# Moving the last store's completion wait to the semaphore clear, and issuing the bulk store one reduction earlier, in a row-sum kernel

## The chip, the cores and the metric

The kernel runs on one core of one Trainium2 chip. The metric is the device time of one execution in microseconds (us). Timed runs of two kernels are taken in turn on the same chip.

A timed run is about 1.8 us longer than the span that the trace shows for it. Differences inside the span carry over; the absolute numbers don't.

The views of the profile name the engines PE (TensorE), DVE (VectorE), ACT (ScalarE), POOL (GpSimd) and SP (SyncE); a q behind the name, as in SPq, means that engine's instruction queue, and L148 is line 148 of that kernel's file. A *semaphore* is a counter that some instructions change and others wait for. A transfer has *landed* when the last of the 16 additions to its semaphore is on record (for the last store of the kernel before they run from 159.983 to 160.151 us). A *barrier* is a point that every engine must reach before any of them goes on. A *drain* is a DRAIN instruction of the trace; here it matters only as an instruction that a wait can stand on. The *span* runs from the start of the first instruction in the trace to the end of the last.

## The reference

```python
batch, seq, dim = 32, 512, 1024
def reference(x):                       # x: (32, 512, 1024) float32
    return np.sum(x, axis=-1).astype(np.float32)
```

67.1 MB are read once, and 64 KB of sums are written.

## The kernel before

The 16,384 rows are cut into eight groups. In each, a partition holds 16 whole rows, so a full load is 8 MB. All loads are issued by SyncE, in order, into three buffers. VectorE reduces the groups; from the seventh group on, ScalarE takes some of the rows. The last group is loaded in shrinking pieces (8 rows, 5 rows, 2 rows, and one row in two parts) so that little work is left when the last bytes land. Results leave by two stores: the *group store* (seven groups, 896 pieces of 64 bytes, issued by ScalarE) and the *last store* (the eighth group, 128 pieces of 64 bytes, issued by SyncE).

```python
def rows(t, a, n, j, n_act, pairs=False):
    nv = n - n_act
    block = t[:, a * dim : (a + n) * dim].rearrange("p (n d) -> p n d", d=dim)
    load = nc.sync.dma_start(out=block, in_=rows_from(j, n))
    ...                                  # nv rows to VectorE, n_act rows to ScalarE
    return load
# ... groups 0 to 6 ...
rows(t, 0, 8, j, 4)
rows(t, 8, 5, j + 8, 2, pairs=True)
rows(t, 13, 2, j + 13, 1, pairs=True)    # the "two-row load"
# ...
nc.vector.memset(whole[:, width + 1 :], 0.0)
nc.sync.dma_start(out=part, in_=rows_from(j, 1)[:, 0, :c])
nc.sync.dma_start(out=whole[:, 1 : width + 1], in_=rows_from(j, 1)[:, 0, c:])
hold(store(nc.scalar, 0, last), sums_of[-1], "its packets come behind those of the loads")
halves(whole[:, :1], part)
halves(sums[:, j : j + 1], whole)
store(nc.sync, last, last + 1)
```

`hold(a, b)` makes `a` wait for `b`. So the group store waits for VectorE's sum of the two-row load.

The framework adds a closing block behind this. In the kernel before, cut to what matters:

```
SyncE    waits for every load, both stores and all engines' counts; the last
         of these waits (the last store) stands on a drain
all      first barrier: each engine's drain adds 1; GpSimd gathers 4, then releases 4
GpSimd   drain
GpSimd   clear of the semaphores
GpSimd   drain
all      second barrier, the same way
```

A second hook of the kernel, `order_waits`, only orders the waits of one instruction. It sorts the last store's wait to the front of the drain's list; in the trace that wait then stands on the drain itself (160.167 us), and the other waits on instructions ahead of it.

## Time and profile before

| | before |
|---|---|
| median of the first three runs | 162.2 us (161.96 to 162.31) |
| span of the trace | 160.9 us |
| loads, share of the chain that ended last | 73% |
| VectorE's long reductions, share of the same chain | 24% |
| last load landed to last store issued | 0.48 us |
| last store issued to landed | 1.42 us |
| last store landed to the clear | 0.365 us |
| last store landed to the end of the span | 0.75 us |

The page of the kernel before gives the span, then the chain of waits by engine and line, then groups of instructions: busy us, mean ns of one, idle time before them and what ended it.

```profile
span 160.9 us, 126 instructions
...
DMA t<-in_x_dram 73%; DVE sums L98 24%; SPq L137 1%; SPq L178 0%; DVE t L112 0%; DVEq L209 0%
...
L98 DVE TENSOR_REDUCE sums<-t 128x16 f32<-128x16384 f32 (+3 forms) x9 | 116.6, 12953 | 36.2 <-DMA t<-in_x_dram 36.2
```

The packets of SyncE's DMA queue, nearly all of them loads, take up 97.6% of the 16 DMA engines' time, so the kernel is paced by its loads; by this chain, what can still gain are the loads themselves or what comes after them.

The timeline of the kernel before shows the end (start us, duration us, engine, line, operation). Shown are VectorE's sum of the two-row load's last row, the group store on ScalarE's queue, VectorE's very last sum, and the last store on SyncE's queue.

```profile
156.96 0.69 DVE L112 CUSTOM_DVE_ANT_0 t<-t 128x512 f32<-128x512 f32 x1 [0.58 <-DMA t<-in_x_dram]
...
157.69 0.41 ACTq L148 DMA_DIRECT2D out_dram<-sums  x1
...
158.30 0.40 DVE L112 CUSTOM_DVE_ANT_0 t<-t 128x233 f32<-128x233 f32 x1
158.62 0.08 DVE L112 DVE_READ_ACCUMULATOR2_ANT sums<- 128x1 f32 x1
158.74 0.35 SPq L148 DMA_DIRECT2D out_dram<-sums  x1
```

The group store is released 0.73 us after VectorE starts on the two-row load's last sum. After the last store's issue no engine computes, yet the span goes on to 160.9: that is the store's flight and the closing block.

SyncE's waits of the kernel before (waiter, what it waited for: total us, times, longest us) say what it does there.

```profile
SPq L209 <- DMA out_dram<-sums: 0.8, 2, 0.5
SPq L209 <- PEq L209: 0.6, 2, 0.4
```

It waits for both stores ("2"), and only then enters the barriers (the second line; the view puts those waits down to TensorE's queue, but in the raw records they end behind GpSimd's release, in the first barrier at 160.378 us, 0.042 us after the release started). The views leave out the semaphore instructions of the closing block; their times below come from the raw event records of the same trace.

### The profile page before, as it was taken

Reading aid. Unit: us, or ns where it says so; the run is one execution under the profiler, and the core shown is the slowest. Engines: PE = TensorE matmul, PEld = TensorE weight load, DVE = VectorE, ACT = ScalarE, POOL = GpSimd, SP = SyncE. Lnnn points to the kernel's source line nnn. Section 1 sums busy time; section 2 is a strip of 40 time slices with the busy share of each in tenths; the row PEclk is TensorE's granted clock in tenths of the full one; section 3 lists DMA queues with packets and bytes.
Section 4 is the critical chain, followed back from the end, with each engine's and each line's share of the span. In section 5 each row is a group of like instructions: output and inputs, shape, how many; then the busy total and the mean of one; then the engine's idle time right before and its main releaser. Section 6 shows DMA issues by size and latency. Waiting matters only on the chain.

```text
span 160.9 us, 126 instructions
## 1 busy us (share of the span) xinstructions
DVE 120.1 (75%) x22; ACT 17.3 (11%) x31; POOL 0.2 (0%) x4
## 2 busy tenths in 40 slices
DVE  0280069950799958999499994999949999597943
ACT  3000000000000000000000000000000000596952
POOL 0000000000000000000000000000000000000000
DMA  7999996996996969969969969969969969999993
GB/s 265 452 477 501 391 521 261 521 521 261 521 521 261 521 261 521 521 261 521 521 261 521 521 261 521 521 261 521 521 261 521 521 261 521 391 391 424 407 406 82
DMA packets 2929, 67.18 MB, mean 418 GB/s; under 512 B 1265, under 2 KB 1393, under 8 KB 1521
## 3 DMA queue, kind: packets, MB, share of 16 engines
q1 hardware_dynamic: 2016, 67.12, 97.6%
q10 hardware_dynamic: 912, 0.06, 0.4%
q14 instruction: 1, 0.00, 0.0%
HBM read 67.11 MB, written 0.07 MB: 417 GB/s over the span
## 4 chain that ended last, share of the span: by engine, by line
DMA 73%; DVE 24%; SPq 1%; issue 0%; DVEq 0%
DMA t<-in_x_dram 73%; DVE sums L98 24%; SPq L137 1%; SPq L178 0%; DVE t L112 0%; DVEq L209 0%
## 5 line engine op out<-in xcount | busy, mean ns | idle before, releaser
L98 DVE TENSOR_REDUCE sums<-t 128x16 f32<-128x16384 f32 (+3 forms) x9 | 116.6, 12953 | 36.2 <-DMA t<-in_x_dram 36.2
L125 ACT ACTIVATE unread<-t 128x1024 f32<-128x1024 f32 x15 | 15.2, 1013 | 140.0 <-DMA t<-in_x_dram 140.0
L112 DVE CUSTOM_DVE_ANT_0 t<-t 128x512 f32<-128x512 f32 (+2 forms) x6 | 3.5, 601 | 2.4 <-DMA t<-in_x_dram 2.3
L125 ACT ACTIVATION_READ_ACCUMULATOR unread<-t 128x1 f32 x15 | 2.8, 188 | 0.0
L125 ACT ACT_TABLE_LOAD x1 | 1.3, 1283 | 0.8 <-PEq L198 0.8
L112 DVE DVE_READ_ACCUMULATOR2_ANT sums<- 128x1 f32 x5 | 0.4, 82 | 0.0
L198 POOL MEMSET const-bfloat16-1.0<- 128x1 bf16 x1 | 0.1, 102 | 0.0
L198 POOL MEMSET const-uint8-127<- 128x1 uint8 x1 | 0.1, 101 | 0.0
L198 POOL MEMSET const-float32-0.0<- 128x1 f32 x1 | 0.1, 99 | 0.2 <-issue 0.2
L198 POOL MEMSET const-float32-1.0<- 128x1 f32 x1 | 0.1, 98 | 0.0
L112 DVE DVE_READ_ACCUMULATOR2_ANT t<- 128x1 f32 x1 | 0.1, 82 | 0.0
L176 DVE MEMSET t<- 128x1 f32 x1 | 0.1, 59 | 0.0
## 6 DMA issues: line engine op xcount, KB each, us to landing
t<-in_x_dram SPq DMA_DIRECT2D x1, 6144.0 KB, 20.8
t<-in_x_dram SPq DMA_DIRECT2D x1, 4096.0 KB, 31.1
t<-in_x_dram SPq DMA_DIRECT2D x1, 2560.0 KB, 36.9
t<-in_x_dram SPq DMA_DIRECT2D x1, 2048.0 KB, 7.1
t<-in_x_dram SPq DMA_DIRECT2D x1, 1024.0 KB, 38.9
t<-in_x_dram SPq DMA_DIRECT2D x1, 280.0 KB, 39.2
t<-in_x_dram SPq DMA_DIRECT2D x1, 232.0 KB, 39.3
t<-in_x_dram SPq DMA_DIRECT2D x6, 41.2
```

The costliest lines, as they stand in the source:

```text
L98: return nc.vector.tensor_reduce(out=dst, in_=src, axis=mybir.AxisListType.X, op=mybir.AluOpType.add)
L112: return nc.vector.tensor_tensor_reduce(out=src[:, :n], in0=src[:, :n], in1=src[:, n:], scale=1.0, scalar=0.0, op0=mybir.AluOpType.add, op ...
L125: nc.scalar.activation(out=unread[:, :n], in_=src, func=mybir.ActivationFunctionType.Copy, accum_out=dst,)
L137: load = nc.sync.dma_start(out=block, in_=rows_from(j, n))
L176: nc.vector.memset(whole[:, width + 1 :], 0.0)
L198: nc = _bacc.Bacc("TRN2", target_bir_lowering=False, num_devices=1)
```

## The change

The intent is to let the first closing barrier run while the last store is still in flight. SyncE no longer waits for that store; GpSimd does, on the drain that already stands between the first barrier and the clear. The clear is kept behind the landing, because it also acts on the semaphore that the store increments (in the trace before, that semaphore changes at 160.566 us, 0.05 us after the clear starts). That a clear ahead of the landing would do harm is reasoning. The group store's hold moves from VectorE's sum to the two-row load itself, so that SyncE, which still waits for the group store ahead of the barrier, is early enough.

```diff
 def order_waits(nc):
...
-            elif isinstance(inst, mybir.InstDrain) and inst.engine == SP:
-                insts[k] = with_first(inst, stored)
...
+def wait_for_the_store_at_the_clear(nc):
+    ...                       # take `wait` (the last store) off SyncE's drain
+    insts[at] = copy.replace(
+        insts[at], sync_info=mybir.SyncInfo(on_wait=rest, on_update=info.on_update)
+    )
+    pool = [k for k, i in enumerate(insts) if i.engine == mybir.EngineType.Pool]
+    clear = next(k for k in pool if isinstance(insts[k], mybir.InstISA))
+    drain = pool[pool.index(clear) - 1]
+    ...                       # checks that this drain waits for nothing yet
+    insts[drain] = copy.replace(
+        insts[drain], sync_info=mybir.SyncInfo(on_wait=[wait], on_update=[])
+    )
...
-        rows(t, 13, 2, j + 13, 1, pairs=True)
+        two = rows(t, 13, 2, j + 13, 1, pairs=True)
...
-        hold(store(nc.scalar, 0, last), sums_of[-1], "its packets come behind those of the loads")
+        hold(store(nc.scalar, 0, last), two, "its packets come behind those of the loads")
```

The source adds no instruction to any engine.

More of the change, by code (lines that the diff above doesn't have):

```diff
@@ L42, in order_waits @@
     SP = mybir.EngineType.SP
-    stored = None
     for block in nc.main_func.blocks:
@@ L52, in order_waits @@
                 insts[k] = with_first(inst, "DVE")
-                stored = inst.sync_info.on_update[0].ant_name
-            elif isinstance(inst, mybir.InstDrain) and inst.engine == SP:
-                insts[k] = with_first(inst, stored)
         block.instructions = insts
+def wait_for_the_store_at_the_clear(nc):
+    end = nc.main_func.blocks[-1]
+    insts = list(end.instructions)
+    stored = [
+        i.sync_info.on_update[0].ant_name
+        for b in nc.main_func.blocks
+        for i in b.instructions
+        if isinstance(i, mybir.InstDMACopy) and i.engine == mybir.EngineType.SP
+    ][-1]
+    at = next(
+        k
+        for k, i in enumerate(insts)
+        if isinstance(i, mybir.InstDrain) and i.engine == mybir.EngineType.SP
+    )
+    info = insts[at].sync_info
+    (wait,) = [w for w in info.on_wait if w.ant_name == stored]
+    rest = [w for w in info.on_wait if w.ant_name != stored]
+    insts[at] = copy.replace(
[4 more added lines that the diff above has]
+    drain = pool[pool.index(clear) - 1]
+    assert isinstance(insts[drain], mybir.InstDrain)
+    info = insts[drain].sync_info
+    assert info is None or not (info.on_wait or info.on_update)
+    insts[drain] = copy.replace(
+        insts[drain], sync_info=mybir.SyncInfo(on_wait=[wait], on_update=[])
+    )
+    end.instructions = insts
 @with_exitstack
@@ L68 @@
     nc.at_finalize(order_waits)
+    nc.at_finalize(wait_for_the_store_at_the_clear)
     fp32 = mybir.dt.float32
```

## The prediction

> **What bounds the kernel now.** The chain of waits gives 73% of the 160.9 us span to the loads of x and 24% to VectorE's long reductions, which free the buffers of later loads. The change touches neither; it acts on the last 4 us only. There the raw events of the trace read: two-row load landed 156.93; last load landed 158.26; last two-piece sum on VectorE done 158.72; last store (SyncE) issued 158.74, its 128 packets 159.57 to 159.78, landed 160.15. Group store (ScalarE): issued 157.69, released by VectorE's sum at 157.67; its 896 packets 158.64 to 159.38, landed 159.80. After the last landing comes a serial tail: SyncE's drain wakes 160.17, second drain 160.23, GpSimd gathers 160.26, releases 160.34, drains 160.42, clears the semaphores 160.52, and a second barrier ends at 160.9.
>
> **What the change does.**
> 1. SyncE no longer waits for the last store, so the first closing barrier runs while that store is in flight; GpSimd's existing drain in front of the clear takes the wait. From landing to clear it was 160.516 - 160.151 = 0.365 us. What remains is the wake (0.016 us, as SyncE's drain shows) and drain to clear (160.516 - 160.417 = 0.099 us): 0.115 us. Gain 0.25 us, all on the critical path. The second barrier is paced by GpSimd before and after (the other engines' drains end at 160.55, GpSimd's gather starts 160.72), so the shift passes through whole. No instruction is added to any engine.
> 2. SyncE's wait for the group store remains, ahead of the barrier. At the old landing (159.80) SyncE would reach its barrier at about 160.0 and GpSimd its drain at about 160.19, 0.02 to 0.04 us late: the early group store covers that. In the built program the dependency on the two-row load vanishes, since ScalarE's preceding activation already waits for it; the issue follows at about 156.98, 0.71 us earlier. With the same 0.95 us from issue to first packet its packets run 157.94 to 158.66, landing near 159.1. SyncE then passes everything by about 159.45 and GpSimd stands at its wait from about 159.7, some 0.45 us ahead of the landing.
>
> **The cost to fear.** The early packets could run into the last loads: their last data packet ends at 157.81, only 0.13 us before the first expected store packet. [...] I expect none or a few hundredths. The last store's own packets meet no group packets before or after, so its 1.41 us from issue to landing should stand.
>
> **Predicted time.** 162.2 - 0.25 = 161.95 us. The three runs of before spread over 0.35 us, as much as the gain, so the 8-in-10 range is 161.6 to 162.3. Faster by over 2%: 0.005; within 2%: 0.99; slower: 0.005.
>
> **What would show each step.** Timeline of the tail: group store issued at about 157.0; SyncE's drains before 159.6; GpSimd's first gather before 159.7; its drain 0.02 us after the last landing; the clear 0.1 to 0.13 us after that landing instead of 0.37. The last load's landing should stay 1.3 us behind the two-row load's, the last store's issue to landing 1.4 us.
>
> **What would make it wrong.** [...] a drain of GpSimd that wakes more slowly from a DMA's semaphore than SyncE's; a second barrier not paced by GpSimd; or run-to-run drift of the loads, which moves more than the tail.

Two passages are cut from this text: a mechanism by which early store packets would delay the last load, with an upper bound for it, and the same mechanism in the list of what would make it wrong. No run of this case shows that mechanism. No term of the sum was in them: the forecast is 162.2 - 0.25 = 161.95 us, with nothing added for a collision. "None or a few hundredths" is what the author expected of that delay.

## The result

| | before | after |
|---|---|---|
| median of 6 runs | 162.12 us (161.94 to 162.47) | 161.91 us (161.72 to 162.35) |
| ratio | 1 | 0.9988 (95% interval 0.9971 to 1.0005) |

A ratio is the mean time of one kernel's runs over that of the other's of the same rounds, so it is not quite the ratio of the medians quoted beside it. The medians came out 0.21 us apart. These twelve runs alone do not prove a gain: the interval includes 1.

The same page lines for the changed kernel (all line numbers have moved by the inserted code, L98 to L130 and so on):

```profile
span 160.2 us, 125 instructions
...
DMA t<-in_x_dram 73%; DVE sums L130 24%; SPq L169 1%; SPq L210 0%; DVE t L144 0%; DVEq L241 0%
...
L130 DVE TENSOR_REDUCE sums<-t 128x16 f32<-128x16384 f32 (+3 forms) x9 | 116.6, 12953 | 35.5 <-DMA t<-in_x_dram 35.5
```

The span is 0.65 us shorter, more than was predicted, and a reader should not book all of it: the long reductions are just as busy (116.6 us) but waited 0.7 us less for loads, which the change does not touch. (0.3 us of that comes back in front of the sums of the last small pieces, whose waits grew from 2.3 to 2.6 us, so the loads as a whole were about 0.4 us faster.) The traced execution of the kernel before was also a slow one of its kind: it took 162.69 us, more than any of its six timed runs.

The timeline of the changed kernel:

```profile
156.56 0.69 DVE L144 CUSTOM_DVE_ANT_0 t<-t 128x512 f32<-128x512 f32 x1 [0.58 <-DMA t<-in_x_dram]
156.62 0.41 ACTq L180 DMA_DIRECT2D out_dram<-sums  x1
...
157.88 0.40 DVE L144 CUSTOM_DVE_ANT_0 t<-t 128x233 f32<-128x233 f32 x1
158.21 0.08 DVE L144 DVE_READ_ACCUMULATOR2_ANT sums<- 128x1 f32 x1
158.32 0.35 SPq L180 DMA_DIRECT2D out_dram<-sums  x1
```

The group store now leaves 0.06 us after the two-row load's sum has started (0.73 us before). The last stretch, from VectorE's last half to the last store, is 0.44 us in both.

SyncE's waits of the changed kernel in the closing block:

```profile
SPq L241 <- PEq L241: 1.1, 2, 0.9
```

The line that waited for `out_dram` is gone. SyncE now waits longer inside the barriers (0.6 to 1.1 us): it is there early.

The raw event records of the two traces, in us from the start of each span:

| event | before | after |
|---|---|---|
| five-row load landed | 154.42 | 154.02 |
| two-row load landed | 156.93 | 156.54 |
| last load landed | 158.26 | 157.84 |
| group store: issued, packets, landed | 157.69, 158.64 to 159.38, 159.80 | 156.62, 157.54 to 158.28, 158.72 |
| last store: issued, packets, landed | 158.74, 159.57 to 159.78, 160.151 | 158.32, 159.16 to 159.37, 159.744 |
| SyncE's drain of the first barrier | 160.23 | 159.04 |
| GpSimd gathers, releases | 160.26, 160.34 | 159.07, 159.15 |
| GpSimd's drain in front of the clear starts | 160.417 | 159.768 |
| the clear starts | 160.516 | 159.867 |
| end of the span | 160.899 | 160.250 |

Of the last store's 1.42 us in the kernel before, 0.84 us pass from the start of the issue to the first packet (0.49 us from its end), 0.21 us are packets, and 0.37 us pass from the last packet to the landing.

Four terms add up to the 0.65 us. The last load landed 0.417 us earlier; the way from there to the last store's issue took 0.002 us more; the store's flight took 0.008 us more; landing to end fell from 0.748 to 0.506 us, by 0.242 us. The first term is not the change's: 0.40 of the 0.417 us was already there when the five-row load landed, before either edit acts. Over the thirteen traces the last load lands anywhere from 157.42 to 158.26 us.

### The profile page after: what moved, and what is told of

The parts are those of the page before. It is cut to its first block, busy times and chain, and to the rows that moved or that the text cites. A ratio compares the mean times of both kernels' runs of the same rounds, so it can differ in the third digit from the quotient of the medians.

```text
span 160.2 us, 125 instructions
## 1 busy us (share of the span) xinstructions
DVE 120.1 (75%) x22; ACT 17.3 (11%) x31; POOL 0.2 (0%) x4
## 4 chain that ended last, share of the span: by engine, by line
DMA 73%; DVE 25%; SPq 1%; issue 0%; DVEq 0%
DMA t<-in_x_dram 73%; DVE sums L130 24%; SPq L169 1%; SPq L210 0%; DVE t L144 0%; DVEq L241 0%
## 5 line engine op out<-in xcount | busy, mean ns | idle before, releaser
L130 DVE TENSOR_REDUCE sums<-t 128x16 f32<-128x16384 f32 (+3 forms) x9 | 116.6, 12953 | 35.5 <-DMA t<-in_x_dram 35.5
```

Of the source, the lines that this page charges most:

```text
L130: return nc.vector.tensor_reduce(out=dst, in_=src, axis=mybir.AxisListType.X, op=mybir.AluOpType.add)
```

## The experiments

Two measures carry the verdicts: the *tail*, from the last landing of a store to the clear and to the end of the span, and the ratio to the kernel before. All kernels gave the correct result. Each kernel was timed six times, three of them (the group store late, among the last loads, and earlier still) four times. The kernel before ran 11 times on each of three chips, beside the kernels of that chip.

### The kernel before against itself

No edit.

> The kernel before against itself, on one chip with the three runs that follow. Every theory expects a ratio of 1.000; how far it is off, and how wide its interval is, says what a difference of 0.15% in the others is worth. In its trace the last landing comes 0.365 us before the clear, as in the first profile, while the landing of the last load may move by 0.4 us, as it did between the two profiles, if that is drift.

Measured: 162.31 us against 162.03 us, ratio 1.001 (0.999 to 1.003). Landing to clear 0.366 us, landing to end 0.749 us. The last load landed at 157.91 us, 0.34 us earlier than in the first trace of the very same kernel. So the loads drift by nearly as much as the unexplained part of the spans, and a single ratio from some six runs is good to about 0.2% either way. The tail repeats to 0.001 us.

### The change again, twice

No edit.

> The change again, in more rounds. My theory (the gain is the barrier taken out from behind the last landing): landing to clear 0.12 us against 0.365 us, 0.24 us off the time, a ratio of 0.9985. Rival (the 0.2 us between the medians is drift of the loads, which landed 0.4 us earlier in the second profile): a ratio of 1.000.

> The change a third time, beside the next run on one chip. Landing to clear 0.12 us, landing to end 0.51 us in its trace; ratio to the kernel before 0.9985 by the tail alone, with an interval of some 0.15% to either side.

Measured: ratios 0.9991 (0.9972 to 1.0009) and 0.9977 (0.9961 to 0.9994). In both traces landing to clear is 0.123 us and landing to end 0.506 us. With 0.9988 of the first comparison, the three ratios have a mean of 0.9985, which is 0.24 us of 162.2. Two of the three intervals include 1; taken together as independent, they give an estimate of about 0.9975 to 0.9995 for the mean. The rival, drift alone, does not explain the tail, and it would put all three ratios below 1 only one time in eight.

### The wait at the clear alone

```diff
-        hold(store(nc.scalar, 0, last), two, ...)
+        hold(store(nc.scalar, 0, last), sums_of[-1], ...)
```

> The wait at the clear alone; the group store stays behind VectorE's sum. My theory: group store lands 0.35 us before the last store, SyncE then needs 0.19 us to its barrier and GpSimd 0.19 us more to its drain, which is 0.03 us after the last landing: landing to clear 0.15 us, 0.21 us off the time, ratio 0.9987. Rival (the early group store is what gains): landing to clear as before, ratio 1.000.

Measured: landing to clear 0.161 us, landing to end 0.544 us, ratio 0.9993 (0.9971 to 1.0016), too wide to decide. The tail decides: this half of the change gives 0.205 of the 0.243 us. SyncE's waits of this kernel show what still holds it:

```profile
SPq L241 <- DMA out_dram<-sums: 0.6, 1, 0.6
```

One wait is left, for the group store, which landed at 159.07, 0.35 us before the last store (159.42). From there GpSimd's drain started at 159.479, 0.062 us after the last landing instead of 0.024 us in the change.

### The early group store alone

The kernel before, with its hold moved to `two`.

> The early group store alone; SyncE's drain waits for the last store as before. My theory: nothing is gained, landing to clear 0.365 us, issue of the last store to its landing 1.41 us, ratio 1.000. Rival (the early group store clears the way of the last store): issue to landing under 1.3 us and a ratio of 0.9985 or so.

Measured: landing to clear 0.366 us, landing to end 0.749 us, last store 1.414 us from issue to landing, ratio 1.0001 (0.9984 to 1.0018). SyncE's waits of this kernel:

```profile
SPq L209 <- DMA out_dram<-sums: 0.7, 1, 0.7
```

Again one wait, but this time for the last store. The early store by itself buys nothing. Together with the moved wait it is worth 0.544 - 0.506 = 0.038 us.

### The group store held until VectorE's last sum

```diff
-        hold(store(nc.scalar, 0, last), two, ...)
         halves(whole[:, :1], part)
-        halves(sums[:, j : j + 1], whole)
+        total = halves(sums[:, j : j + 1], whole)
+        hold(store(nc.scalar, 0, last), total, ...)
```

> The wait at the clear as in the change, but the group store held until VectorE's last sum, so issued beside the last store. My theory: the group store is still waited for ahead of the first closing barrier, so it now lands last, about 2.1 us after its issue, and the whole barrier comes behind it: landing of the group store to clear 0.45 to 0.5 us, 0.9 to 1.1 us slower than the change, ratio to the kernel before 1.004 to 1.006. Rival (with the wait at the clear the group store's time no longer matters): ratio 0.9985.

Measured: 162.98 us, ratio 1.005 (1.0033 to 1.0066). SyncE's waits of this kernel:

```profile
SPq L241 <- DMA out_dram<-sums: 1.7, 1, 1.7
```

Both stores were issued at 157.91; the last store landed at 159.38, the group store at 160.07. The whole first barrier came behind the group store: 0.509 us from its landing to the clear, 0.892 us to the end. So the wait that the change left on SyncE still counts: the tail got shorter where the group store landed 1.02 us (the change) or 0.35 us (the run with the wait alone) ahead of the last one, and longer here, where it landed 0.69 us behind it. The 0.509 us was 0.01 us over what was expected.

### The group store among the last loads

```diff
-        rows(t, 8, 5, j + 8, 2, pairs=True)
+        five = rows(t, 8, 5, j + 8, 2, pairs=True)
+        hold(store(nc.scalar, 0, last), five, ...)
...
-        hold(store(nc.scalar, 0, last), two, ...)
```

> The change with the group store issued about 1.1 us earlier still, on ScalarE ahead of the two-row load's activation. My theory: its 56 packets of 10 ns on each DMA engine now run among the last loads' packets, and the last load lands 0.3 to 0.9 us later against the five-row load's landing (3.9 us before), of which 0.55 us is the packets' own time: ratio 1.001 to 1.004. Rival (small packets slip in between for nothing, so the order never mattered): the last load's landing stays within 0.1 us and the ratio is that of the change, 0.9985.

Measured: 162.15 us, ratio 1.0003 (0.9983 to 1.0024). The timings from the five-row load's landing say more: the last load's data packets end 3.42 us later, inside the 3.32 to 3.43 us of the kernels with the store behind the loads, but it *lands* 3.956 us later, against 3.804 to 3.835 us there. Sorted in order of time, its 16 completion packets (of 4 bytes) took 0.61 us from packet to landing on average, against 0.44 to 0.50 us there. So there is a cost, of 0.12 to 0.15 us, and it is smaller than the 0.3 us or more that I expected. The rival (under 0.1 us) misses too, by little.

Two parts of the expectation failed. First, ScalarE's sequencer (its instruction queue, ACTq) ran ahead of its engine: the store was issued at 154.14, while ScalarE was busy until 156.3 with the sums that stand before it in the program. That is only 0.09 us after the five-row load landed, about 2.5 us earlier than in the change, not 1.1 us. Second, it then waited. The profile's list of issues (the `--dma` view; size, us to landing) has for the two stores:

```profile
out_dram<-sums ACTq DMA_DIRECT2D x1, 56.0 KB, 4.4
out_dram<-sums SPq DMA_DIRECT2D x1, 8.0 KB, 1.4
```

The first packet came 2.89 us after the issue (0.92 us in the change), at 157.02, so only the last 0.45 us of load packets had store packets beside them.

### The group store earlier still

```diff
-        rows(t, 0, 8, j, 4)
+        eight = rows(t, 0, 8, j, 4)
+        hold(store(nc.scalar, 0, last), eight, ...)
...
-        hold(store(nc.scalar, 0, last), two, ...)
```

> The change with the group store issued some 3 us earlier than in the run amid the loads, behind ScalarE's sums of the eight-row load. There the first packet came 2.89 us after the issue, against 0.92 us in the change. Theory A (on each DMA engine the packets of ScalarE's queue wait until the loads already queued by SyncE have nearly run out): the first packet comes again only about 3.0 us behind the five-row load's landing, so 5 to 7 us after the issue, and the last load lands 0.10 to 0.25 us later than in the change, as in that run. Theory B (a fixed delay of about 2.9 us while loads run): the packets run 3 us earlier, well inside the loads, and the data packets of the last load end up to 0.5 us later behind the five-row load's landing (3.42 us in both traces).

Measured: 162.07 us, ratio 0.9991 (0.9967 to 1.0014), which with this interval says nothing. The list of issues of this kernel:

```profile
out_dram<-sums ACTq DMA_DIRECT2D x1, 56.0 KB, 10.3
out_dram<-sums SPq DMA_DIRECT2D x1, 8.0 KB, 1.4
```

Issued at 147.93 (again ahead of ScalarE's four sums of the eight-row load, which stand before it in the program and took 4.3 us in the trace of the kernel before; so about 6 us earlier than in the run before), first packet at 151.69, last at 157.72. Neither theory fits in full. The first packet came neither 5 to 7 us (A) nor about 2.9 us (B) after the issue, but 3.76 us; B is nearer, as the packets did run inside the loads. Packets of the two queues started at these counts in quarters of a microsecond, over all 16 DMA engines:

```
from us       154.0 154.25 154.5 154.75 155.0 155.25 155.5
load, 8 KB       12     12    12     14    13     13    11
store, 64 B      12     14    11     13    14     12    14
```

From 151.5 to 153.0, while the loads' packets are 20 KB, the six quarters have 3, 12, 1, 3, 11 and 2 load packets, and exactly as many store packets. So in all these quarters about as many store packets started as load packets, and the store was slower beside the loads' larger packets: 32 of its packets in the six quarters beside 20 KB, against 11 to 14 in each quarter beside 8 KB. The trace does not say which DMA engine a packet ran on, so what makes the counts equal was not shown. Nor was the cause of the first delay, 3.76 us here and 2.89 us above; that stays open. The cost is again small: the last load's data ends 3.56 us behind the five-row load's landing (3.32 to 3.43), and it lands after 3.912 us (3.804 to 3.835), so 0.08 to 0.11 us later.

### The wait on the clear itself

```diff
-    drain = pool[pool.index(clear) - 1]
-    ...
-    insts[drain] = copy.replace(
-        insts[drain], sync_info=mybir.SyncInfo(on_wait=[wait], on_update=[])
-    )
+    insts[clear] = copy.replace(
+        insts[clear], sync_info=mybir.SyncInfo(on_wait=[wait], on_update=[])
+    )
```

> The change with the wait moved one instruction further, from GpSimd's drain to the clear itself, so that the drain is over by the landing. My theory: landing to clear 0.02 to 0.03 us in place of 0.12 us, another 0.10 us off, ratio to the kernel before 0.998. Rival (what follows the wake is not paced by GpSimd): the end of the span stays 0.5 us after the last landing.

Measured: landing to clear 0.024 us, landing to end 0.406 us, ratio 0.9989 (0.9973 to 1.0005). The 0.100 us arrives in the tail in full; the ratio cannot resolve it from the change's.

### The second barrier's gather ahead of the clear as well

In addition to the edit above, after the clear has been found:

```diff
+    after = pool[pool.index(clear) + 1 :]
...
+    gather = insts.pop(after[1])
...
+    insts.insert(clear, gather)
```

The other engines already stand in the second barrier, so GpSimd can collect them while the store flies (in the first of these two traces at 159.46, the store landing at 159.80). The release still follows the clear and its drain.

> As the run before it, and GpSimd's gather of the second barrier also stands ahead of the clear, so only clear, drain and release come after the landing. My theory: another 0.08 us off, last landing to the end of the span 0.33 us (0.75 us in the kernel before, 0.51 us in the change), ratio to the kernel before 0.9975. Rival: as in the run before it, 0.5 us.

> The kernel with wait on the clear and the gather ahead of it, again, as it beat the kernel before by 0.26% once, of which its tail accounts for 0.27% (0.435 us). Theory: ratio 0.9973 again, and 0.19 us under the change of the run before this one. Rival (that figure was half luck): ratio over 0.9985.

Measured: landing to end 0.313 and 0.314 us; 161.69 and 161.67 us; ratios 0.9974 (0.9959 to 0.9989) and 0.9974 (0.9957 to 0.9992). This is the fastest version and beats the kernel before beyond noise, twice. Its tail is 0.435 us shorter, 0.27% of 162.2 us, and the timed runs show 0.26%. Against the change, its tail is 0.19 us shorter; on the one chip where both ran, the means of six runs each differ by 0.05 us only (161.77 and 161.82), which neither shows nor refutes 0.19 us, so over the change the gain rests on the tail alone.

| kernel | landing to clear, us | landing to end, us | ratio to before |
|---|---|---|---|
| before (two traces) | 0.365, 0.366 | 0.748, 0.749 | 1, 1.001 |
| early group store alone | 0.366 | 0.749 | 1.0001 |
| wait at the clear alone | 0.161 | 0.544 | 0.9993 |
| the change (three traces) | 0.123, 0.123, 0.123 | 0.506, 0.506, 0.506 | 0.9988, 0.9991, 0.9977 |
| wait on the clear itself | 0.024 | 0.406 | 0.9989 |
| and the gather ahead of it (two traces) | 0.024, 0.024 | 0.313, 0.314 | 0.9974, 0.9974 |

## Why the prediction was right

The predicted time was 161.95 us, the measured median 161.91 us, with the class "within 2%" at 0.99. That the two agree within 0.04 us is partly luck, and the time alone would be weak evidence: the runs of one kernel spread by more than the gain, and the kernel before measured 162.12 us in these rounds, not the 162.2 us that the prediction started from. The steps can be checked one by one in the tail, which does not drift.

- *Landing to clear from 0.365 to 0.115 us, a gain of 0.25 us.* Measured 0.123 us and 0.242 us, in three traces of three. The terms were right: GpSimd's drain started 0.024 us after the landing (0.016 us was taken from SyncE's drain), and drain to clear was 0.099 us before and after. The wait is not part of the drain's recorded time: the drain is 0.070 us long in both traces, though it started 0.081 us after GpSimd's release of the barrier in the kernel before and 0.619 us after it (159.149 us) in the changed kernel. By these figures GpSimd stood in front of it for some 0.5 us, an estimate.
- *The second barrier is paced by GpSimd, so the shift passes through.* Clear to end is 0.383 us before and after. The gather put ahead of the clear then removed another 0.093 us, as it should if only GpSimd was late.
- *The early group store covers 0.02 to 0.04 us and gains nothing else.* 0.038 us with the moved wait, nothing without it.
- *SyncE's barrier drain well ahead of the landing.* 159.04 against a landing at 159.744. GpSimd could start its wait some 0.5 us early, near the 0.45 us of the prediction.
- *The cost to fear did not occur.* In the changed kernel the last load landed 1.30 us behind the two-row load (1.32 before). Its last data packet ended at 157.44, the first store packet started at 157.54, a gap of 0.10 us where 0.13 was expected. The two runs with the store moved forward show what a collision costs here: the last load landed 0.08 to 0.15 us later.

How an early store makes the last load land later was not shown. With the store among the last loads, the last load's completions took longer from packet to landing (0.61 us, against 0.44 to 0.50 us with the store behind the loads), beside a store that took about 0.7 us from its completion packets to its landing. In the run with the store earlier still, with store packets between those of the last loads, they took 0.36 us, less than in any other, and yet the last load landed 0.08 to 0.11 us later. So the longer completions are seen in one of the two runs only.

## What to carry to other kernels

Here a closing barrier that started only when the last store had landed cost 0.24 us; let it run during the store's flight, and let only the semaphore clear wait for the landing. Put in front of that wait everything that the engine can do without it (here the drain, 0.100 us, and the second gather, 0.093 us), and check that every wait left ahead of the barrier ends well before the last landing (here 0.35 us ahead left out 0.038 us of the gain). For gains of a quarter of a per cent, time a stretch of the trace that does not drift (here from the last landing to the end, repeatable to 0.001 us) rather than the whole span, and put the kernel before against itself to see what timed runs can tell.
